# A hybrid attention and RWKV block in fp32 on one core: four products of the recurrent stage pinned behind other dense matmuls, bonus rows loaded sooner, weight casts queued behind evacuations

## The chip, the cores and the metric

The kernel runs on 1 core of one Trainium2 chip. The metric is the device time of that core in microseconds (us) for one execution; of several runs the median is given.

## The reference

One layer of a streaming encoder, on 2048 tokens with 1024 features, all in fp32:

```
h   = RMSNorm_pre(x)
P   = h @ w_in                     # columns: attention q/k/v, RWKV r/k/v + low-rank w/a/g, gates
yA  = chunk-band attention         # own chunk of 64 + 8 previous, bias on clipped distance, 8 heads of 64
yB  = RWKV-7 time mixing           # 8 heads of 64, a scan over time:
        sa    = state @ aa_t
        state = state * w_t + sa b_t^T + v_t k_t^T
        y_t   = state @ r_t
        then a group norm, a bonus (sum(r k r_k) v) and a gate g
m   = sigmoid(gA) * (yA @ proj_a) + sigmoid(gB) * (yB @ proj_b)
x   = x + RMSNorm_post(m @ w_out)
x   = x + RMSNorm_post2(relu(RMSNorm_pre2(x) @ w_up)^2 @ w_down)
```

## The kernel before

The 2048 tokens are done in four groups of 512. For each group three stages follow each other: the recurrent stage (`phase_rwkv`), attention (`phase_attention`) and the merge (`phase_merge`). Behind the fourth group come the two halves of the FFN, which the change leaves alone.

**Dense blocks.** A product of h with 128 columns of w_in is a dense block (`dense`, L108). To keep fp32 accuracy each operand is split into a high and a low part, and a block is 24 matmuls of 128x512 into one PSUM bank `psd`: eight h-high by w-high (hh,whi), eight h-low by w-high (hl,whi), eight h-high by w-low (hh,wlo). The weights of a block are loaded by SyncE's queue (`wraw`), cast to the high part by ScalarE (`whi`, L78) and subtracted to the low part by VectorE (`wlo`, L79). Each of these tiles has two buffers, and so has `psd`. So a block's cast can start only when TensorE is done with the block two back, and a block's matmuls only when the PSUM bank of the block two back has been emptied (evacuated). A group has 30 dense blocks in the recurrent stage (14 that the recurrence needs, `mix`, and 16 gates, `gate`) and 12 in attention (for each of four head pairs Q, K and V, `att_pair`), 168 in all. The branch projections (`branch`, L1086) are split in the same way, for two blocks at a time.

**The recurrent stage.** Eight heads are done as four pairs p, in two blocks b of two pairs. For each pair `rwkv_pre` forms the inputs: `mix` blends a dense block with the token before, the low-rank products `ps_z` and `ps_a` (L391, L392) give decay and rate, `ps_ss` (L450) the norm of k, `ps_v` and `ps_bk` transposes, and `ps_A` (L548) the products within chunks of 64. `rwkv_inverse` inverts small triangles on VectorE, 31 steps for both pairs at once (L584, L590, then the transposes L593 and L595). `rwkv_blocks` completes the inverse with two sets of 32x32 products, `ps_t` at L615 and at L623, which ScalarE empties to Z (L618) and XT (L628). `rwkv_trans` makes the matrices of the chunks: the transposes `ps_at` (L643), four chunks in each of two halves h, then `ps_w`, `ps_ug`, `ps_tq`, `ps_y` and the start states (L684). `rwkv_chunk` runs the recurrence over eight chunks c: `ps_st` (L699) and `ps_y` (L701) on TensorE, and the state ST (L702) on VectorE, which the next chunk needs. Nearly all these small products take turns in two PSUM buffers (`self.pa`), those of the chunks in two others (`self.pr`). `rwkv_post` norms the result (yq, var, grs, yn), adds the bonus rows `bv` (L736, L737; they were written to memory earlier) and multiplies by the gate `ps_g` (L740).

**The order.** Each engine works off one queue in order. A scheduler makes these queues; it may take instructions in another order than the program has them. In the recurrent stage the small products stand between dense matmuls, which fill TensorE while the other engines work for the small ones. Where a small product is to stand is fixed for a few of them: `place(mm, n)` notes that a product comes behind the group's dense matmul number n, and `placed` makes it an order dependency that has no semaphore (`queue_behind`). `BLOCKS` holds these numbers for the first products of L615 and L623, for both blocks b. The other small products come where the scheduler puts them. The order of SyncE's transfers, of the casts and of the evacuations follows from the scheduler too.

Of the kernel before, what the change touches and what calls it, by code (L numbers as in the profile page):

```python
# [9 lines left out]
F32 = mybir.dt.float32  # L10
BF16 = mybir.dt.bfloat16
F32R = mybir.dt.float32r
AF = mybir.ActivationFunctionType
ALU = mybir.AluOpType
# [18 lines left out]

GATES = (0, 0, 1, 0, 0, 0, 0, 1)
STEPS = (1, 2, 1, 1, 1, 1, 1, 1, 1, 1, 1, 0, 0, 2, 1)
BLOCKS = ((412, 424), (623, 632))
BONUS = {(0, 1): 138, (1, 0): 258}
SCORES = 150
DEC = math.exp(-0.5)
# [14 lines left out]
class Block:  # L54
# [50 lines left out]
    def w_in(self, col):  # L105
        return self.a["w_in"][:, col : col + P].rearrange("(k p) n -> p k n", p=P)

    def dense(self, col):  # L108

        first = bool(self.raws)  # L110
        wh, wl = self.wsplit(self.w_in(col), "w", KB, P)
        if first:
            self.queue_behind(self.high.ins, self.highs[2 - len(self.raws)])
            self.queue_behind(self.low, self.last_low)
        ps = self.pd.tile([P, G], F32, tag="d", name="psd")
        self.mm = self.mm3(ps, [(wh[:, k], wl[:, k], self.h[0][:, k], self.h[1][:, k]) for k in range(KB)], True)
        if first:
            self.queue_behind(self.mm[0], self.last_transpose)
        self.dl += self.mm
        return ps  # L120
# [235 lines left out]
    def mix(self, g, blk, out):  # L356

        nc, tp = self.nc, self.tp
        ps = self.dense(RW0 + blk * P)
        pr = tp.tile([P, G + 1], F32, tag="pr", bufs=1, name="pr")  # L360
        nc.scalar.copy(pr[:, 1 : G + 1], ps)
        nc.gpsimd.tensor_copy(pr[:, 0:1], self.carry[:, blk : blk + 1])
        nc.gpsimd.tensor_copy(self.carry[:, blk : blk + 1], pr[:, G : G + 1])
        nc.scalar.activation(out, ps, AF.Copy, scale=self.omu[:, blk : blk + 1])
        nc.vector.scalar_tensor_tensor(
            out, pr[:, 0:G], self.mu[:, blk : blk + 1], out, op0=ALU.mult, op1=ALU.add
        )
# [264 lines left out]
    def rwkv_trans(self, p, R):  # L632

        nc, xp = self.nc, self.xp
        AR, SV, XT, BR = (R[x] for x in ("AR", "SV", "XT", "BR"))
        rows = [slice(0, C), slice(C, P)]
        halves = [slice(0, 4), slice(4, 8)]

        WA = xp.tile([P, NC, 2, C], F32, tag="WA", bufs=1, name="WA")
        for h, cs in enumerate(halves):  # L640
            ps = self.pa.tile([P, 4, P], F32, tag="a", name="ps_at")
            for j in range(4):
                nc.tensor.transpose(ps[:, j], AR[:, h * 4 + j, 0:2].rearrange("p s t -> p (s t)"), self.ident)  # L643
            for par in range(2):
                nc.scalar.copy(WA[rows[par], cs, 0], ps[rows[par], :, par * C : par * C + C])
        ps = self.pa.tile([P, NC, C], F32, tag="a", name="ps_w")
        for c in range(NC):
            for par in range(2):
                ow = rows[1 - par]
                nc.tensor.matmul(ps[rows[par], c], AR[ow, c, par], SV[ow, c, par], start=True, stop=True)  # L650
        nc.scalar.copy(WA[:, :, 1], ps)
        yield

        GT = xp.tile([P, NC, C], F32, tag="GT", bufs=1, name="GT")
        for h, cs in enumerate(halves):
# [36 lines left out]
    def rwkv_chunk(self, p, c, R):  # L692
# [3 lines left out]
        ps = self.pr.tile([P, C], F32, tag="wus", name="ps_st")  # L696
        rows = [slice(0, C), slice(C, P)]
        for r in rows:
            nc.tensor.matmul(ps[r], TQ[r, c, 0], S[r], start=True, stop=True)  # L699
        for r in rows:  # L700
            nc.tensor.matmul(Y[r, c], TQ[r, c, 1], S[r], start=False, stop=c == NC - 1)  # L701
        nc.vector.scalar_tensor_tensor(  # L702
# [4 lines left out]
    def rwkv_post(self, p, R):  # L707
# [10 lines left out]
        nc.gpsimd.tensor_tensor(rs, var, self.nhalf, ALU.pow)  # L718
        yn = self.tmp("yn").rearrange("p (c t) -> p c t", t=C)
        nc.vector.tensor_tensor(yn, Y, rs[:, :, None].to_broadcast((P, NC, C)), ALU.mult)  # L720
        yield
        yf = self.tmp("yf")
        yf3 = yf.rearrange("p (c t) -> p c t", t=C)
        for h in range(2):
# [7 lines left out]
            nc.scalar.activation(  # L732
                yf3[C:P, cs], ps[:, :, C:P], AF.Identity, scale=self.gwo[:, col], bias=self.gbo[:, col]
            )
        bv = self.tmp("bv")
        nc.sync.dma_start(bv, self.bvd[p])  # L736
        self.tc.keep_in_program_order(nc.vector.tensor_tensor(yf, yf, bv, ALU.add))  # L737
        ps = self.py.tile([P, G], F32, tag="y", name="ps_g")
        self.mm3(ps, [(*(x[:, pc] for x in self.g2), *self.lg)])
# [3 lines left out]
    def gate(self, i):  # L743
        nc = self.nc
        ps = self.dense(GATE0 + i * P)
        t = self.sp.tile([P, G], F32, tag="gate", bufs=2, name="gate")
        nc.scalar.activation(t, ps, AF.Tanh, scale=0.5, bias=self.hgb[:, i : i + 1])
        nc.scalar.dma_start(self.gd[i], t)

    def phase_rwkv(self, g, quads):  # L750
# [125 lines left out]
    def att_pair(self, g, p, beside):  # L876
# [12 lines left out]
        for par in range(2):  # L889
            rw, ow = rows[par], rows[1 - par]  # L890
            nc.scalar.activation(QA[rw, par], ps[rw], AF.Copy, scale=-0.125)
            nc.scalar.activation(QB[ow, par], ps[rw], AF.Copy, scale=-0.125)
            for dst in (QB[rw, par], QA[ow, par]):
                nc.vector.scalar_tensor_tensor(  # L894
                    dst, ps[rw], -0.125, QA[rw, par].bitcast(F32), op0=ALU.mult, op1=ALU.subtract
                )
        ps = self.dense(ATT0 + HW + p * P)
        for par in range(2):
            rw, ow = rows[par], rows[1 - par]
            nc.scalar.copy(KK[rw, par, 1], ps[rw])  # L900
            nc.vector.tensor_tensor(KK[ow, par, 1], ps[rw], KK[rw, par, 1].bitcast(F32), ALU.subtract)
        ps = self.dense(ATT0 + 2 * HW + p * P)
        vf = ap.tile([P, G], F32, tag="vf", bufs=1, name="vf")
        nc.scalar.copy(vf, ps)
        pst = self.pt.tile([P, GT, P], F32, tag="t", name="ps_vt")
        for t in range(GT):
            nc.tensor.transpose(pst[:, t], vf[:, t * P : (t + 1) * P], self.ident)
# [178 lines left out]
    def branch(self, y, br, i):  # L1086

        nc, mp = self.nc, self.bp
        t = mp.tile([P, G], F32, tag="th", bufs=3, name="th")
        nc.sync.dma_start(t, self.gd[br * KB + i])  # L1090
        if i % 2 == 0:
            w = self.a[("proj_a", "proj_b")[br]][:, i * P : (i + 2) * P]
            self.bw = self.wsplit(w.rearrange("(k p) n -> p k n", p=P), "w", NP, 2 * P)
        wh, wl = (x[:, :, i % 2 * P : (i % 2 + 1) * P] for x in self.bw)
        ps = self.pd.tile([P, G], F32, tag="d", name="ps_p")
        self.mm3(ps, [(wh[:, k], wl[:, k], y[0][:, k], y[1][:, k]) for k in range(NP)])
        nc.vector.scalar_tensor_tensor(t, t, 1.0, ps, op0=ALU.add, op1=ALU.mult)  # L1097
        return t

    def phase_merge(self, g, o, op, between, beside):  # L1100
# [380 lines left out]
    def run(self):  # L1481
        tc, e = self.tc, None
        with ExitStack() as ctx, ExitStack() as mixing:
            e = mixing.enter_context
            consts = self.constants(ctx, mixing)
            advance(consts, 1)
            self.pd = ctx.enter_context(tc.tile_pool(name="pd", bufs=2, space=PSUM))
            self.wp = e(tc.tile_pool(name="w", bufs=2))
# [89 lines left out]
```

## Time and profile before

| | |
|---|---|
| time, median of 3 runs | 3269.18 us (3267.48 to 3270.03) |
| time of the profiled execution | 3272.55 us |
| its span | 3270.8 us |
| mean granted clock of TensorE | 0.993 |
| TensorE busy, matmuls | 3184.3 us |
| VectorE, ScalarE, GpSimd busy | 2239.5, 1576.9, 596.0 us |
| first group: recurrent stage's last dense matmuls to attention's first scores | near 300 to 314 us |
| second group: first recurrence, second recurrence, attention | from near 620, 719, 785 us |

Engines are named as in the profile: PE is TensorE (its matmuls), PEld TensorE's weight loads, DVE VectorE, ACT ScalarE, POOL GpSimd, SP SyncE, whose queue issues most DMAs. A row of a timeline gives the start and the time in us, engine, line and operation, out<-in, shapes, and how many instructions it stands for; what follows in brackets is the time that the engine was idle ahead of it, and the instruction whose end ended that. A row of a group of instructions (part 5 of the page) gives the busy time and the mean ns of one, and then the idle time of the engine ahead of them. A row of the windows gives for a stretch of the span the busy time of each engine, the clock that TensorE was granted (1.00 is full speed), the share of the DMA engines and GB/s. The trace counts some matmuls of the small products twice as often as the program (x32 for 16).

### The profile page before, as it was taken

What the parts mean: (1) busy time and instruction counts of PE and PEld (TensorE: products, weight loads), DVE (VectorE), ACT (ScalarE), POOL (GpSimd) and SP (SyncE); (2) the same over time, 40 slices, a digit from 0 to 9 for tenths busy, and PEclk for the clock granted to TensorE, in tenths of its full rate; (3) what the DMA queues carried; (4) which work ended last, traced back from release to release, by engine and by line L of the source; (5) the groups of instructions that cost most, each with busy time, mean ns of one, the idle gap of its engine ahead of it and who ended that gap; (6) DMA issues with size and microseconds to landing.
All of it is one profiled execution on the core that took longest, in us unless ns stands there. A gap on an engine that the chain in (4) does not pass through costs nothing. (4 is left out here: it accounts for less than half of the span.)

```text
span 3270.8 us, 50026 instructions
## 1 busy us (share of the span) xinstructions
PE 3184.3 (97%) x18913; PEld 2599.2 (79%) x18913; DVE 2239.5 (68%) x3655; ACT 1576.9 (48%) x2511; POOL 596.0 (18%) x1101
## 2 busy tenths in 40 slices
PE   8999999999999999999999999999999999999998
PEld 6777778777888777878877887888888878888887
DVE  7785666776776785776866775887656768775464
ACT  5434635445745434755434653544543444544343
POOL 2221012122112222112222110122211212120000
PEclk9999999999999999999999999999999999999999
DMA  5245373246574236565336547654777875456565
GB/s 167 85 135 172 126 241 119 72 142 235 181 234 133 88 120 234 182 205 170 94 97 206 182 156 238 226 182 166 254 278 248 290 238 193 167 177 229 193 217 175
DMA packets 432282, 592.54 MB, mean 181 GB/s; under 512 B 25300, under 2 KB 295840, under 8 KB 432040
## 3 DMA queue, kind: packets, MB, share of 16 engines
q1 hardware_dynamic: 373928, 408.94, 39.9%
q0 software_dynamic: 48896, 163.61, 13.7%
q10 hardware_dynamic: 9216, 16.78, 1.4%
q8 instruction: 149, 2.44, 0.3%
q14 instruction: 93, 0.76, 0.1%
HBM read 425.37 MB, written 167.01 MB: 181 GB/s over the span
## 5 line engine op out<-in xcount | busy, mean ns | idle before, releaser
L1409 PE MATMUL ps_dn<-fop 128*128 128x512 f32 x2688 | 611.9, 389 | 1.8 <-DVE fop L79 1.7
L1409 PEld LDWEIGHTS ps_dn<-fop 128*128 128x128 f32 x2688 | 504.0, 188 | 107.8 <-DVE fop L79 2.8
L78 ACT CAST whi<-wraw 128x1024 fp32r<-128x1024 f32 x232 | 243.5, 1050 | 392.9 <-PE psd L88 301.1
L88 PE MATMUL psd<-hh,whi 128*128 128x512 f32 x1344 | 370.3, 403 | 10.7 <-DVE QA L894 10.7
L79 DVE TENSOR_TENSOR wlo<-wraw,whi 128x1024 fp32r<-128x1024 f32 x232 | 283.0, 1220 | 133.3 <-ACT whi L78 70.0
L88 PE MATMUL psd<-hl,whi 128*128 128x512 f32 x1344 | 367.2, 401 | 0.0
L88 PE MATMUL psd<-hh,wlo 128*128 128x512 f32 x1344 | 358.4, 398 | 0.0
L88 PEld LDWEIGHTS psd<-hh,whi 128*128 128x128 f32 x1344 | 244.8, 190 | 59.8 <-issue 11.8
L88 PEld LDWEIGHTS psd<-hl,whi 128*128 128x128 f32 x1344 | 249.1, 190 | 49.5
L88 PEld LDWEIGHTS psd<-hh,wlo 128*128 128x128 f32 x1344 | 247.9, 189 | 50.8 <-issue 1.4
L79 DVE TENSOR_TENSOR fop<-xraw,fop 128x1024 fp32r<-128x1024 f32 x112 | 137.0, 1224 | 178.9 <-ACT fop L78 178.7
L78 ACT CAST fop<-xraw 128x1024 fp32r<-128x1024 f32 x112 | 117.8, 1052 | 256.4 <-PE ps_dn L1409 186.3
L1286 POOL DMA_DIRECT2D xd<-X x192 | 104.2, 545 | 384.2 <-ACT X L1283 321.9
L79 DVE TENSOR_TENSOR fop<-wdraw,fop 128x1024 fp32r<-128x1024 f32 x112 | 136.6, 1220 | 19.0 <-ACT fop L78 18.8
L78 ACT CAST fop<-wdraw 128x1024 fp32r<-128x1024 f32 x112 | 117.7, 1051 | 34.8 <-DMA wdraw<-in_w_down_dram 20.0
L947 DVE CUSTOM_DVE_ANT_0 sc<-bias,ps_s 128x640 f32<-128x640 f32 (+4 forms) x128 | 93.8, 732 | 54.2 <-PE ps_pt L958 27.1
L963 DVE TENSOR_TENSOR PTl<-ps_pt,PTh 128x640 fp32r<-128x640 f32 (+4 forms) x128 | 94.5, 738 | 32.7 <-ACT PTh L962 31.2
L78 ACT CAST s12h<-s 128x1024 fp32r<-128x1024 f32 x32 | 33.7, 1053 | 163.0 <-PE ps_u L88 163.0
L88 PE MATMUL ps_p<-yh,whi 128*128 128x512 f32 x256 | 102.6, 405 | 6.0 <-DVE th L1097 5.3
L962 ACT CAST PTh<-ps_pt 128x640 fp32r<-128x640 f32 (+4 forms) x128 | 79.7, 623 | 55.2 <-PE ps_pt L958 54.6
L952 ACT ACTIVATE sc<-sc,mn 128x640 f32<-128x640 f32 (+4 forms) x128 | 97.8, 764 | 17.4 <-DVE mn L947 15.4
L1126 PE MATMUL ps_o<-whi,mh 128*128 128x512 f32 x256 | 101.4, 396 | 1.8 <-DVE o L1137 1.8
(369 smaller groups left out, 6848.9 us busy)
## 6 DMA issues: line engine op xcount, KB each, us to landing
wraw<-in_w_in_dram SPq DMA_DIRECT2D x168, 512.0 KB
xraw<-xd SPq DMA_DIRECT2D x112, 512.0 KB
xd<-X POOLq DMA_DIRECT2D x192, 256.0 KB, 5.2
wraw<-in_w_up_dram SPq DMA_DIRECT2D x80, 512.0 KB
wdraw<-wd SPq DMA_DIRECT2D x64, 512.0 KB
wdraw<-in_w_down_dram SPq DMA_DIRECT2D x48, 512.0 KB
gd<-gate ACTq DMA_DIRECT2D x64, 256.0 KB
wd<-cmb POOLq DMA_DIRECT2D x64, 256.0 KB, 4.3
```

Source lines behind the costliest of these rows:

```text
L78: high = self.high = self.nc.scalar.copy(hi, src)
L79: self.low = self.nc.vector.tensor_tensor(lo, src, hi.bitcast(F32), ALU.subtract).ins
L88: mm.append(nc.tensor.matmul(ps, l, r, start=n == 0, stop=n == last).ins)
L947: nc.vector.tensor_tensor_reduce(sc[:, 0:n], bias[:, s0:640], pss[:, c0 : c0 + n], 1.0, 3.0e38, ALU.add, ALU.min, mn,)
L952: nc.scalar.activation(sc[:, 0:n], sc[:, 0:n], AF.Exp, scale=-1.0, bias=mn, accum_out=sm[:, col : col + 1])
L962: nc.scalar.copy(hv, pst[:, 0:nk])
L963: nc.vector.tensor_tensor(lv, pst[:, 0:nk], hv.bitcast(F32), ALU.subtract)
L1126: nc.tensor.matmul(ps[t], l[:, k, ts], r[:, k % 2], start=k == 0 and j == 0, stop=k == KB - 1 and j == 2)
L1286: nc.gpsimd.dma_start(self.xd[q][i // 2][:, i % 2], src)
L1409: nc.tensor.matmul(ps, o[:, l, k, sl], o[:, r, k], start=start and n == 0, stop=stop and n == end)
```

## The change

Five edits; what is computed stays the same, and so does the number of instructions on each engine.

1. TURNED: the first transpose of the second half of `ps_at`, for the first pair, is placed behind dense matmul 438.
2. FIFTH: the first product of chunk 4 of the first pair is placed behind dense matmul 494.
3. BLOCKS: for the second block of pairs the two sets of `ps_t` are placed behind 631 and 644 instead of 623 and 632.
4. The load of the bonus rows `bv` stands ahead of the first pause of `rwkv_post`, instead of behind the transposes that follow that pause.
5. `follow`: every evacuation of a dense block (or of a branch product) is noted in `emptied`. The cast of a block's high part is queued on ScalarE behind ScalarE's evacuation of the block three back, and the subtraction of its low part on VectorE behind VectorE's, where there is one. This is again an order without a semaphore.

```diff
-BLOCKS = ((412, 424), (623, 632))
+BLOCKS = ((412, 424), (631, 644))
+TURNED = 438
+FIFTH = 494
...
+    def follow(self):
+
+        for ins, done in zip((self.high.ins, self.low), self.emptied[-3] if len(self.emptied) > 2 else ()):
+            if done is not None:
+                self.queue_behind(ins, done.ins)
...
     def dense(self, col):
...
+        self.follow()
         ps = self.pd.tile([P, G], F32, tag="d", name="psd")
...
-        nc.scalar.activation(out, ps, AF.Copy, scale=self.omu[:, blk : blk + 1])
+        self.emptied.append((nc.scalar.activation(out, ps, AF.Copy, scale=self.omu[:, blk : blk + 1]), None))
...
             for j in range(4):
-                nc.tensor.transpose(ps[:, j], AR[:, h * 4 + j, 0:2].rearrange("p s t -> p (s t)"), self.ident)
+                mm = nc.tensor.transpose(ps[:, j], AR[:, h * 4 + j, 0:2].rearrange("p s t -> p (s t)"), self.ident)
+                if p == 0 and h == 1 and j == 0:
+                    self.place(mm, TURNED)
...
-            nc.tensor.matmul(ps[r], TQ[r, c, 0], S[r], start=True, stop=True)
+            mm = nc.tensor.matmul(ps[r], TQ[r, c, 0], S[r], start=True, stop=True)
+            if p == 0 and c == 4 and r.start == 0:
+                self.place(mm, FIFTH)
...
         nc.vector.tensor_tensor(yn, Y, rs[:, :, None].to_broadcast((P, NC, C)), ALU.mult)
+        bv = self.tmp("bv")
+        nc.sync.dma_start(bv, self.bvd[p])
         yield
...
-        bv = self.tmp("bv")
-        nc.sync.dma_start(bv, self.bvd[p])
         self.tc.keep_in_program_order(nc.vector.tensor_tensor(yf, yf, bv, ALU.add))
...
-        nc.scalar.activation(t, ps, AF.Tanh, scale=0.5, bias=self.hgb[:, i : i + 1])
+        self.emptied.append((nc.scalar.activation(t, ps, AF.Tanh, scale=0.5, bias=self.hgb[:, i : i + 1]), None))
...
-            nc.scalar.activation(QB[ow, par], ps[rw], AF.Copy, scale=-0.125)
+            act = nc.scalar.activation(QB[ow, par], ps[rw], AF.Copy, scale=-0.125)
...
-                nc.vector.scalar_tensor_tensor(
+                dve = nc.vector.scalar_tensor_tensor(
...
+        self.emptied.append((act, dve))
...
             self.bw = self.wsplit(w.rearrange("(k p) n -> p k n", p=P), "w", NP, 2 * P)
+            self.follow()
```

The evacuations of K and V and of the branch products are noted in the same way. How the rows move on the queues, at three places; a row gives the line in its own kernel, so that L643 of before is L652 of after, and so on.

The first place is TensorE's queue in the first recurrence. Before, between the two halves of the first pair's transposes:

```order
103 L623 MATMUL ps_t_1474<-XT,Z 32x32 x32
104 L643 MATMUL ps_at<-ident,AR 128x128 x4
105 L88 MATMUL psd<-hh,wlo 128x512 x4
106 L643 MATMUL ps_at<-ident,AR 128x128 x4
107 L650 MATMUL ps_w<-SV,AR 64x64 x16
```

The same place now:

```order
103 L632 MATMUL ps_t_1474<-XT,Z 32x32 x32
104 L652 MATMUL ps_at<-ident,AR 128x128 x4
105 L90 MATMUL psd<-hh,wlo 128x512 x7
106 L90 MATMUL psd<-hh,whi 128x512 x7
107 L652 MATMUL ps_at<-ident,AR 128x128 x4
108 L661 MATMUL ps_w<-SV,AR 64x64 x16
```

Fourteen dense matmuls stand between the halves where four stood. Further on the same queue, around chunk 0 (whose state is st_99 and st_100), the low-rank products and chunk 1, before:

```order
144 L391 MATMUL ps_z<-lora,whw 128x512
145 L392 MATMUL ps_z<-lora,wlw 128x512
146 L88 MATMUL psd<-hh,wlo 128x512 x4
147 L391 MATMUL ps_a<-lora,wha 128x512
148 L392 MATMUL ps_a<-lora,wla 128x512
149 L88 MATMUL psd<-hh,wlo 128x512 x3
150 L699 MATMUL ps_st<-st_99,TQ 64x64 x2
151 L701 MATMUL ps_y<-st_99,TQ 64x64 x2
152 L699 MATMUL ps_st<-st_100,TQ 64x64 x2
153 L701 MATMUL ps_y<-st_100,TQ 64x64 x2
154 L88 MATMUL psd<-hh,whi 128x512 x4
155 L699 MATMUL ps_st<-ST,TQ 64x64 x2
```

And now:

```order
146 L710 MATMUL ps_st<-st_100,TQ 64x64 x2
147 L714 MATMUL ps_y<-st_100,TQ 64x64
148 L400 MATMUL ps_z<-lora,whw 128x512
149 L401 MATMUL ps_z<-lora,wlw 128x512
150 L714 MATMUL ps_y<-st_100,TQ 64x64
151 L400 MATMUL ps_a<-lora,wha 128x512
152 L401 MATMUL ps_a<-lora,wla 128x512
153 L710 MATMUL ps_st<-ST,TQ 64x64 x2
154 L714 MATMUL ps_y<-ST,TQ 64x64 x2
155 L710 MATMUL ps_st<-ST,TQ 64x64 x2
156 L714 MATMUL ps_y<-ST,TQ 64x64 x2
157 L90 MATMUL psd<-hh,whi 128x512 x8
```

The dense matmuls that stood between these products are gone from there, and chunk 0 comes ahead of the low-rank products. Chunk 4, with FIFTH, comes 24 dense matmuls behind `ps_ss` in both kernels.

The second place is the start and the end of the second block's inverse. On TensorE the two sets of `ps_t`, before:

```order
230 L88 MATMUL psd<-hh,wlo 128x512 x8
231 L615 MATMUL ps_t_2553<-X_2451,NA 32x32 x32
232 L88 MATMUL psd<-hh,whi 128x512 x8
233 L88 MATMUL psd<-hl,whi 128x512
234 L623 MATMUL ps_t_2588<-XT,Z 32x32 x32
```

And now:

```order
227 L90 MATMUL psd<-hh,whi 128x512 x8
228 L624 MATMUL ps_t_2553<-X_2455,NA 32x32 x32
229 L90 MATMUL psd<-hl,whi 128x512 x8
230 L90 MATMUL psd<-hh,wlo 128x512 x5
231 L632 MATMUL ps_t_2588<-XT,Z 32x32 x32
```

The first set comes eight dense matmuls later, and between the two are 13 instead of 9. VectorE's queue at the start of that inverse (N is its input, T and X its steps; var and yn are the first block's norm), before:

```order
301 L715 TENSOR_REDUCE var<-yq 128x8
302 L574 STREAM_TRANSPOSE N<-NA 128x1024
303 L720 TENSOR_TENSOR yn<-ps_y,grs 128x512
304 L584 TENSOR_TENSOR T<-N,X 128x31
305 L79 TENSOR_TENSOR wlo<-wraw,whi 128x1024
306 L715 TENSOR_REDUCE var<-yq 128x8
307 L590 TENSOR_TENSOR X<-X,T 128x31
308 L79 TENSOR_TENSOR wlo<-wraw,whi 128x1024
309 L720 TENSOR_TENSOR yn<-ps_y,grs 128x512
```

And now:

```order
300 L728 TENSOR_REDUCE var<-yq 128x8
301 L583 STREAM_TRANSPOSE N<-NA 128x1024
302 L733 TENSOR_TENSOR yn<-ps_y,grs 128x512
303 L728 TENSOR_REDUCE var<-yq 128x8
304 L593 TENSOR_TENSOR T<-N,X 128x31
305 L81 TENSOR_TENSOR wlo<-wraw,whi 128x1024
306 L733 TENSOR_TENSOR yn<-ps_y,grs 128x512
307 L599 TENSOR_TENSOR X<-X,T 128x31
308 L81 TENSOR_TENSOR wlo<-wraw,whi 128x1024
```

The second variance moves ahead of a weight cast, and the second yn ahead of another.

The third place is ScalarE's queue where the first Q product of attention is emptied to QA and QB, in two halves. Before:

```order
560 L78 CAST whi<-wraw 128x1024
561 L891 ACTIVATE QA<-psd 64x512
562 L892 ACTIVATE QB<-psd 64x512
563 L78 CAST whi<-wraw 128x1024
564 L891 ACTIVATE QA<-psd 64x512
565 L892 ACTIVATE QB<-psd 64x512
566 L900 CAST KK<-psd 64x512 x2
```

And now:

```order
562 L80 CAST whi<-wraw 128x1024
563 L904 ACTIVATE QA<-psd 64x512
564 L905 ACTIVATE QB<-psd 64x512
565 L904 ACTIVATE QA<-psd 64x512
566 L905 ACTIVATE QB<-psd 64x512
567 L80 CAST whi<-wraw 128x1024
568 L914 CAST KK<-psd 64x512 x2
```

Both halves come ahead of the second cast; VectorE's four operations of L894 come ahead of the next subtraction in the same way.

More of the change, by code (lines that the diff above doesn't have):

```diff
@@ L899, in att_pair @@
             rw, ow = rows[par], rows[1 - par]
-            nc.scalar.copy(KK[rw, par, 1], ps[rw])
-            nc.vector.tensor_tensor(KK[ow, par, 1], ps[rw], KK[rw, par, 1].bitcast(F32), ALU.subtract)
+            act = nc.scalar.copy(KK[rw, par, 1], ps[rw])
+            dve = nc.vector.tensor_tensor(KK[ow, par, 1], ps[rw], KK[rw, par, 1].bitcast(F32), ALU.subtract)
+        self.emptied.append((act, dve))
         ps = self.dense(ATT0 + 2 * HW + p * P)
         vf = ap.tile([P, G], F32, tag="vf", bufs=1, name="vf")
-        nc.scalar.copy(vf, ps)
+        self.emptied.append((nc.scalar.copy(vf, ps), None))
         pst = self.pt.tile([P, GT, P], F32, tag="t", name="ps_vt")
@@ L1096, in branch @@
         self.mm3(ps, [(wh[:, k], wl[:, k], y[0][:, k], y[1][:, k]) for k in range(NP)])
-        nc.vector.scalar_tensor_tensor(t, t, 1.0, ps, op0=ALU.add, op1=ALU.mult)
+        self.emptied.append((None, nc.vector.scalar_tensor_tensor(t, t, 1.0, ps, op0=ALU.add, op1=ALU.mult)))
         return t
@@ L1485, in run @@
             consts = self.constants(ctx, mixing)
+            self.emptied = []
             advance(consts, 1)
```

## The prediction

> **What bounds the kernel now.** I read the page first, then PE's waits, then PE's clock, then what ended the longest waits. From the page, the span, the busy times, and the group of weight casts (its last column is the idle time ahead of them):
>
> ```profile
> span 3270.8 us, 50026 instructions
> PE 3184.3 (97%) x18913; PEld 2599.2 (79%) x18913; DVE 2239.5 (68%) x3655; ACT 1576.9 (48%) x2511; POOL 596.0 (18%) x1101
> L78 ACT CAST whi<-wraw 128x1024 fp32r<-128x1024 f32 x232 | 243.5, 1050 | 392.9 <-PE psd L88 301.1
> ```
>
> PE bounds it: idle only 3270.8 − 3184.3 = 86.5 us. No other engine is near. The casts wait for PE (301.1 us), not PE for the casts. So an edit pays only by taking PE's idle time, or by making PE's busy time run at full clock. PE's waits (line, what it waited for, us in total, times, longest):
>
> ```profile
> PE psd L88 <- DVE QA L894: 10.7, 4, 2.9
> PE ps_at L643 <- ACT XT L628: 9.4, 4, 2.4
> PE ps_t L615 <- DVE X L593: 6.8, 5, 1.7
> ...
> PE ps_st L699 <- DVE ST L702: 5.1, 4, 1.3
> ...
> PE ps_t L623 <- ACT Z L618: 4.7, 8, 0.8
> ```
>
> Each comes about once a group, in the four groups. Together they are 36.7 us, and all five lie where the change moves something. The other 50 us (start, merge, FFN) it leaves as they are.
>
> Some stalls cost twice: PE is at half clock behind them. First three rows of PE's timeline in dense work (8 matmuls each), then the windows behind stalls (us, then busy times by engine, then the granted clock, here 0.57 to 1.00):
>
> ```profile
> 781.30 1.98 PE L88 MATMUL psd<-hl,whi 128*128 128x512 f32 x8
> 783.11 1.98 PE L88 MATMUL psd<-hh,wlo 128*128 128x512 f32 x8
> ...
> 305.85 3.75 PE L88 MATMUL psd<-hh,whi 128*128 128x512 f32 x8 [2.90 <-DVE QA L894]
> ```
>
> ```profile
> 143.00:149.00 6.00, 5.79 (x66) 4.59 (x68) 1.23 (x1) 2.97 (x9) 0.57 (x1) 0.72 0.17 51
> 242.00:249.00 7.00, 7.00 (x112) 5.65 (x108) 0.00 (x0) 3.78 (x8) 0.54 (x1) 0.76 0.78 242
> 305.00:313.00 8.00, 7.15 (x19) 5.70 (x20) 2.07 (x3) 0.96 (x2) 0.70 (x1) 0.57 0.40 131
> ...
> 1131.00:1137.00 6.00, 5.23 (x76) 4.16 (x78) 1.23 (x1) 4.41 (x12) 0.57 (x1) 1.00 0.27 78
> ...
> 1638.00:1645.00 7.00, 6.43 (x74) 5.06 (x74) 1.23 (x1) 3.96 (x10) 0.57 (x1) 0.76 0.21 63
> 1737.00:1743.00 6.00, 5.90 (x107) 4.97 (x108) 0.00 (x1) 2.74 (x8) 0.54 (x1) 0.72 0.95 293
> ```
>
> At full clock eight dense matmuls take 783.11 − 781.30 = 1.81 us, 0.227 each; behind the QA wait of group 0 the same eight took 3.75. What a window loses is its width times (1 − clock): 6 × 0.28 = 1.68, 7 × 0.24 = 1.68, 8 × 0.43 = 3.44. The ps_at stall (143, 1638 and, alike, 625) had one in 3 of 4 groups, not at 1131; the stalls of L615 and L623 had one in 4 of 4 (first 242, last 1737); the QA stall only in group 0, a double one. That is 5.0 + 6.7 + 3.4 = 15.1 us beside the 36.7.
>
> **The change part by part**, with the times of the second group.
>
> *TURNED.* The second four transposes, PE and then ACT:
>
> ```profile
> 621.35 0.66 PE L643 MATMUL ps_at<-ident,AR 128*128 128x128 f32 x4
> 621.76 1.17 PE L88 MATMUL psd<-hh,wlo 128*128 128x512 f32 x4
> 625.29 0.66 PE L643 MATMUL ps_at<-ident,AR 128*128 128x128 f32 x4 [2.36 <-ACT XT L628]
> ```
>
> ```profile
> 623.15 1.04 ACT L78 CAST whi<-wraw 128x1024 fp32r<-128x1024 f32 x1
> 624.08 1.16 ACT L628 COPY XT<-ps_t 32x512 f32<-32x512 f32 x2
> ```
>
> They wait for the PSUM buffer that the two XT copies empty at 625.24; ACT does a whi cast ahead of these. The pin puts 14 dense matmuls between the halves where 4 stood: 10 × 0.227 = 2.27 of the 2.36 us is filled with work that was to come anyway. I leave 0.25 per group: 9.4 becomes 1.0, a gain of 8.4, and with the stall the 5.0 of half clock.
>
> What is late next: those ten were taken from between chunk 0, the two lora products (ps_z, ps_a) and chunk 1, which now follow each other with none between. PE's last ps_A, the last reading of its PSUM buffer, and the scan that stands ahead of chunk 1's ST on DVE:
>
> ```profile
> 655.93 1.16 PE L548 MATMUL ps_A<-AR,BK 64*128 64x128 f32 x8
> ```
>
> ```profile
> 658.21 0.41 DVE L566 TENSOR_TENSOR BR<-ps_A,mN 128x256 f32<-128x256 f32 x1
> ...
> 661.93 1.22 DVE L432 TENSOR_TENSOR_SCAN tw<-reset,tw 128x512 f32<-128x512 f32 x1
> ```
>
> BR ends at 658.62, 1.5 us after the ps_A; chunk 0 (16 small products, about 0.6 us) and ps_z (two of dense size, 0.45) fill some 1.1 of it before ps_a wants the buffer: 0.45. Chunk 2 has nine dense ahead of it (2.0 us), against ST behind a scan of 1.22 and three shorter operations: 0.35. The fourth pair's ps_A now follows a chunk with no dense before it and waits for a BR: 0.4. So 1.2 per group, 4.8 in all. The bounds are nothing, and three waits of the next row's size (3 × 1.29 × 4 = 15.5); I stay with the worked sum, since each part is a difference of quoted ends.
>
> *FIFTH.* PE at chunk 4, and the DVE chain that it waits for, first and last:
>
> ```profile
> 674.74 0.33 PE L699 MATMUL ps_st<-ST,TQ 64*64 64x64 f32 x4 [1.29 <-DVE ST L702]
> ```
>
> ```profile
> 666.45 0.17 DVE L452 TENSOR_SCALAR n2t<-ps_ss 128x8 f32<-128x8 f32 x1 [1.04 <-PE ps_ss L450]
> ...
> 674.32 0.47 DVE L702 SCALAR_TENSOR_TENSOR ST<-ps_st,gC,S 128x64 f32<-128x64 f32 x2
> ```
>
> Chunk 4 is pinned 8 dense later, but ST is queued behind 7.9 us of DVE work that starts at ps_ss, and ps_ss also moves 8 dense later, pulled by the ten above. There are 24 dense between ps_ss and chunk 4 in both. I count no gain; bounds 0 and the whole 5.1.
>
> *BLOCKS.* PE, then DVE's yn, then ACT:
>
> ```profile
> 718.93 1.20 PE L615 MATMUL ps_t<-X,NA 32*32 32x32 f32 x64 [1.64 <-DVE X L593]
> ...
> 723.21 0.24 PE L623 MATMUL ps_t<-XT,Z 32*32 32x32 f32 x2 [0.82 <-ACT Z L618]
> ```
>
> ```profile
> 696.64 0.69 DVE L720 TENSOR_TENSOR yn<-ps_y,grs 128x512 f32<-128x512 f32 x1 [1.81 <-POOL grs L718]
> ```
>
> ```profile
> 720.92 1.05 ACT L78 CAST whi<-wraw 128x1024 fp32r<-128x1024 f32 x1
> ...
> 722.58 0.58 ACT L618 COPY Z<-ps_t 32x512 f32<-32x512 f32 x1
> ```
>
> L615 comes 8 dense later, but the last ps_A, from which DVE's chain of the inverse starts, comes 6 later: net 2 × 0.227 = 0.45 us. The rest must come from DVE. With the casts reordered, its second variance comes ahead of a wlo cast of 1.2 us and the 1.81 us that yn waits for POOL shrink, so the chain is about 1.0 us shorter. 1.64 − 0.45 − 1.0 leaves 0.2: 6.8 becomes 0.8, a gain of 6.0. L623 gets 13 dense behind L615 instead of 9 (+0.91 us), and the cast at 720.92 goes ahead of the XT copies, so Z comes about 1 us sooner: 1.18 is covered, a gain of 4.5 of 4.7. With both the 6.7 of half clock goes. The bounds: the cover alone on L615 (1.8 instead of 6.0) and nothing of the 6.7, or all of it.
>
> *Bonus rows and the Q products.* In the order SP, DVE, ACT, PE:
>
> ```profile
> 773.85 0.51 SPq L736 DMA_DIRECT2D bv<-bvd  x1
> ```
>
> ```profile
> 779.66 0.69 DVE L737 TENSOR_TENSOR yf<-yf,bv 128x512 f32<-128x512 f32 x1 [4.45 <-DMA bv<-bvd]
> ...
> 781.06 1.22 DVE L79 TENSOR_TENSOR wlo<-wraw,whi 128x1024 fp32r<-128x1024 f32 x1
> ...
> 787.15 0.69 DVE L894 SCALAR_TENSOR_TENSOR QA<-psd,QA 64x512 fp32r<-64x512 f32 x1
> ```
>
> ```profile
> 783.31 1.05 ACT L78 CAST whi<-wraw 128x1024 fp32r<-128x1024 f32 x1 [2.42 <-PE psd L88]
> ```
>
> ```profile
> 787.99 2.08 PE L88 MATMUL psd<-hh,whi 128*128 128x512 f32 x8 [2.61 <-DVE QA L894]
> ```
>
> DVE stood 4.45 us for the bonus rows, with wlo and the emptying of the Q product queued behind; then the second half of Q stood behind the whi cast that waited for PE until 783.31, and ended at 787.84. Now the rows are issued ahead of two or three weight loads of SP, and both halves stand ahead of the next cast on ACT and on DVE. From 782.2 (the end of wlo) four operations of 0.69 end near 785, and without the 4.45 nearer 783.7; PE comes at 787.99 − 2.61 = 785.4. The wait goes: 10.7 becomes 0.5, a gain of 10.2, and the 3.4 of half clock. The weight loads are issued up to two DMA issues (0.51 each) later; they are loaded two blocks ahead and none of PE's waits names a load, so nothing is charged. If that cover were gone it is 1 us for each of two loads a group, 8 in all.
>
> *Casts behind evacuations.* No instruction is added. A cast may now stand behind an evacuation that itself waits for PE, and hold what is queued behind it on ACT and DVE. The evacuation of the block three back is due 32 dense matmuls (7.3 us) before the high part is wanted, the cast takes 1.05: some 6 us of slack. I charge nothing where they run on time. It helps where a cast waited at the head:
>
> ```profile
> 657.78 1.05 ACT L78 CAST whi<-wraw 128x1024 fp32r<-128x1024 f32 x1 [11.93 <-PE psd L88]
> ```
>
> There tw and what follows of the lora step stood behind it; now they come first.
>
> **Sum.** −8.4 − 5.0 + 4.8 − 0 − 6.0 − 4.5 − 6.7 − 10.2 − 3.4 = −39.4 us. The profiled execution took 3272.55, 3.37 over the median of 3269.18. So 3269.2 − 39.4 = 3229.8 against the median.
>
> **One rule of the Trainium skill** speaks against 15.1 us of it. The Trainium skill, page "TensorE: Matmul & The Clock Gate", section "Part 1: The HAM clock gate (the "warmup" mystery)", says that the clock drops after at least one idle window of about 3.4 us, a window that runs freely. By that, waits of 1.64 and 2.36 us are too short to cause the half clock. The trace differs so far: the windows above follow such waits. That three of four follow the ps_at stall, and not the one at 1131, fits a freely running window.
>
> **The rivals.**
>
> 1. *The chains move along.* L615 gains only its cover (1.8, not 6.0), L623 3.6 of 4.5, the half clock there stays (6.7): 4.2 + 0.9 + 6.7 = 11.8 less, 3241.6. For it: ps_A does move by 6 dense, and the ps_ss case shows the pattern. Against: a DVE idle of 1.81 that the new order should shrink.
>
> 2. *All goes.* 36.7 + 15.1 = 51.8, and the new waits are hidden: 3217.4. For it: PE still has dense work on both sides of each place. Against: ps_ss moves with chunk 4.
>
> 3. *The half clock stays.* If it belongs to the time and not to the stalls, 15.1 is lost from the sum: 3244.9. The Trainium skill's page "TensorE: Matmul & The Clock Gate" would have it so. Against: the windows quoted above all lie directly behind stalls.
>
> 4. *Slower: casts come late.* Place: every dense block, 42 a group, 168 in all. If an evacuation is held up on ACT or DVE by over 6 us, the cast behind it is late and PE waits, up to a whole cast, 1.05 us. It takes 39.4 + 6.5 = 46 us of that, 44 of the 168 blocks, to be slower by 0.2%; at 70 blocks it is 73 − 39 = 34 slower, 3303. For it: ACT's idle of 11.93 shows that a cast at the head can hold its queue so long. Against: DVE and ACT are 68% and 48% busy.
>
> 5. *Same.* Waits of 1.29 come up at all three crowded places (15.5, not 4.8), together with 1 and with the other half-clock stretches (5.0 + 3.4) staying: 39.4 − 10.7 − 11.8 − 8.4 = 8.5, so 3260.7, and within 0.2% if the Q wait keeps a fifth (2 us) as well.
>
> **How the numbers follow.** 0.2% (6.5 us) is about what a measurement of this kernel tells from no change. Chances: the forecast 0.48 (3223 to 3236), rival 1 0.21, rival 2 0.11, rival 3 0.05, all faster: 0.85. Rival 5 has 0.07, rival 4 has 0.08. The range goes from a few us below rival 2 to 3255, between rivals 1 and 5: 3211 to 3255; outside lie rivals 4 and 5 and little else.
>
> **What would show it.** In the new profile, right: PE's waits lack QA, ps_at is at most 0.5 a group, L615 and L623 together below 1 a group, ps_st still near 1.3 a group, ps_a or ps_A new at 0.3 to 0.5; clocks of 1.00 behind L623. Wrong: a wait of psd for whi or wlo (rival 4); L615 at 1.2 or more with the half clock behind it (rival 1); clock of 0.5 where PE did not stall (rival 3); waits of over 1 us at chunk 1 or 2.

## The result, and the profile after

The changed kernel takes 3245.38 us (median of 4, 3241.73 to 3250.15) against 3269.61 us (median of 4) for the kernel before: a ratio of 0.9929, 95% interval 0.9913 to 0.9945. That is 24.2 us faster, inside the range on record and above the predicted 3229.8. The profiled execution took 3241.73 us, the shortest of the four; its page begins:

```profile
span 3240.0 us, 50025 instructions
...
PE 3169.1 (98%) x18913; PEld 2588.2 (80%) x18913; DVE 2240.5 (69%) x3655; ACT 1575.2 (49%) x2511; POOL 604.0 (19%) x1101
```

The span is 30.8 us shorter. PE's busy time fell by 15.2 and its idle time by 15.6 us, from 86.5 to 70.9: about half of the gain is clock, half is waiting. PE's waits (us in total, times, longest), without that of the start:

```profile
PE ps_yt L742 <- ACT yf L747: 8.0, 4, 2.3
...
PE ps_st L710 <- DVE ST L715: 4.2, 4, 1.1
PE ps_s L956 <- DVE mn L962: 4.2, 6, 1.1
PE ps_p L90 <- ACT yh L80: 3.0, 3, 1.4
...
PE psd L90 <- ACT k L373: 1.1, 4, 0.3
...
PE ps_t L624 <- DVE X L602: 0.7, 2, 0.4
PE ps_a L400 <- DVE BR L575: 0.6, 4, 0.2
```

Of the five waits of before, those of QA, ps_at and Z (L623 of before) are gone, that of X fell from 6.8 to 0.7, that of chunk 4 from 5.1 to 4.2. The longest of these is one that before did not have: ps_yt, 8.0 us, about 2 a group. Attention's ps_s grew from 1.7 to 4.2 and the branch's wait for yh from 0.3 to 3.0.

PE's timeline at the second half of ps_at, which now stands behind 14 dense matmuls and waits for nothing:

```profile
610.94 0.66 PE L652 MATMUL ps_at<-ident,AR 128*128 128x128 f32 x4
611.35 1.89 PE L90 MATMUL psd<-hh,wlo 128*128 128x512 f32 x7
613.08 1.77 PE L90 MATMUL psd<-hh,whi 128*128 128x512 f32 x7
614.88 0.66 PE L652 MATMUL ps_at<-ident,AR 128*128 128x128 f32 x4
```

And at Q, where the dense block that waited 2.61 us follows the scores without a gap:

```profile
768.66 0.30 PE L956 MATMUL ps_s<-KK,QA 128*128 128x320 f32 x1
...
768.95 2.00 PE L90 MATMUL psd<-hh,whi 128*128 128x512 f32 x8
```

The windows of the profile after (the clock is the third number from the end): behind ps_at, behind the second ps_t set, and behind the new wait in the third group:

```profile
614.00:620.00 6.00, 5.85 (x78) 4.39 (x76) 1.03 (x1) 4.33 (x11) 1.26 (x2) 1.00 0.57 168
711.00:718.00 7.00, 6.93 (x130) 5.44 (x130) 1.88 (x3) 4.50 (x9) 1.63 (x3) 1.00 0.96 300
1194.00:1200.00 6.00, 5.95 (x23) 4.59 (x24) 5.35 (x20) 3.26 (x6) 0.54 (x1) 0.72 0.62 194
```

The first two places have full clock. The only half-clock stretch before the end of the span (1.7 us lost) follows the new wait.

Where that wait comes from can be read off the queues of the second group. PE first, then ScalarE, SyncE and VectorE:

```profile
693.49 0.63 PE L742 MATMUL ps_yt<-ident,yn 128*64 128x128 f32 x4 [1.80 <-ACT yf L747]
```

```profile
690.78 1.05 ACT L80 CAST whi<-wraw 128x1024 fp32r<-128x1024 f32 x1 [4.79 <-DMA wraw<-in_w_in_dram]
691.74 0.68 ACT L760 ACTIVATE gate<-psd,hgb 128x512 f32<-128x512 f32 x1
692.32 0.55 ACT L744 ACTIVATE yf<-ps_yt,cst 64x256 f32<-64x256 f32 x1
```

```profile
684.74 0.38 SPq L66 DMA_DIRECT2D wraw<-in_w_in_dram  x1
```

```profile
682.74 0.69 DVE L733 TENSOR_TENSOR yn<-ps_y,grs 128x512 f32<-128x512 f32 x1 [1.82 <-POOL grs L731]
683.47 1.21 DVE L81 TENSOR_TENSOR wlo<-wraw,whi 128x1024 fp32r<-128x1024 f32 x1
```

Read from the bottom: yn waits 1.82 us for GpSimd, and a wlo is queued behind it. That wlo is the last reader of a weight buffer, so the next load is issued at 684.74. The whi cast of that load waits for it until 690.78 at the head of ScalarE's queue, with a gate and the emptying of ps_yt (yf) queued behind. PE waits for yf. It is a chain through four queues.

### The profile page after: what moved, and what is told of

Read it like the earlier page. It is cut to its first block, busy times and chain, and to the rows that moved or that the text cites. A ratio compares the mean times of both kernels' runs of the same rounds, so it can differ in the third digit from the quotient of the medians.

```text
span 3240.0 us, 50025 instructions
## 1 busy us (share of the span) xinstructions
PE 3169.1 (98%) x18913; PEld 2588.2 (80%) x18913; DVE 2240.5 (69%) x3655; ACT 1575.2 (49%) x2511; POOL 604.0 (19%) x1101
## 5 line engine op out<-in xcount | busy, mean ns | idle before, releaser
L90 PE MATMUL psd<-hl,whi 128*128 128x512 f32 x1344 | 358.9, 396 | 0.0
```

The costliest lines, as they stand in the source:

```text
L90: mm.append(nc.tensor.matmul(ps, l, r, start=n == 0, stop=n == last).ins)
```

## The experiments

Each was timed against the kernel before on the same chip; since the times of the kernel before vary by a few us between the chips, ratios are compared. The expectations speak of the time of the changed kernel as 3245. Code is cut at the marks `...`.

**Is it the early bonus rows?** My first reading (theory A) blamed them: they stand ahead of weight loads on SyncE. In `bv_second`, whose edit is shown, only the last two pairs load early; in `no_V` all four load where they did before:

```diff
+        if p > 1:
             bv = self.tmp("bv")
             nc.sync.dma_start(bv, self.bvd[p])
         yield
...
+        if p < 2:
+            bv = self.tmp("bv")
+            nc.sync.dma_start(bv, self.bvd[p])
```

> The changed kernel, but the bonus rows of the first two pairs are loaded where they were before; only those of the last two pairs are loaded early. TensorE's order is the same as in the changed kernel, row for row. Theory A: the 8.0 us that TensorE waits at ps_yt for ACT yf (2.0 a group) come from the early loads, which put the weight loads later in the schedule, so that a cast waits for its DMA at the head of ScalarE's queue with gate and yf behind it; then ps_yt waits at most 0.5 us in all and the time falls by about 8 us, to 3237. Theory B: they come from TURNED, which puts TensorE ten dense matmuls ahead of ScalarE and VectorE; then ps_yt still waits 7 to 8 us and the time stays at 3245.

Measured: 3245.04 us, ratio 0.9929 [0.9915, 0.9943], and ps_yt:

```profile
PE ps_yt L743 <- ACT yf L748: 10.2, 4, 3.6
```

> The changed kernel without any early load of bonus rows (all four pairs as before). Theory A: ps_yt waits at most 0.5 us; the wait for QA stays below 2 us in all, since the casts queued behind the evacuations alone put both halves of Q ahead of the next cast; time 3237 to 3240. Theory B: ps_yt 7 to 8 us, 3245. If it was the early load that took away the wait for QA, 10.7 us of it are back: 3248 under A, 3256 under B.

Measured: 3245.3 us, ratio 0.9932 [0.9919, 0.9944]:

```profile
PE ps_yt L740 <- ACT yf L745: 9.6, 4, 4.4
...
PE psd L90 <- DVE QA L907: 0.6, 2, 0.3
```

Theory A fell: with no early load at all the wait is as long. The wait for QA stays away without the early rows.

**Is it TURNED?** `no_T` leaves out its pin:

```diff
-                if p == 0 and h == 1 and j == 0:
-                    self.place(mm, TURNED)
```

> The changed kernel without TURNED. Both theories: ps_at waits 9.4 us again, with 5 us of half clock; the waits of 1.7 us at psd<-k and ps_a go. Theory A (early loads alone): ps_yt still waits 8 us, so 3245 + 9.4 + 5 - 1.7 = 3258. Theory B, or both edits needed together: ps_yt waits nothing, 3250.

Measured: 3253.05 us, ratio 0.9954 [0.9941, 0.9967]. No row of PE's waits names ps_yt any more, and:

```profile
PE ps_at L652 <- ACT XT L637: 9.4, 4, 2.4
...
PE ps_t L624 <- DVE X L602: 4.5, 5, 1.0
```

So the wait at ps_yt comes with TURNED. Without it the order on VectorE changes too: each wlo stands ahead of the yn that waits. And the cover of BLOCKS alone does not suffice for X: 4.5 us are left there and 2.6 for Z (L615 and L623 of before).

**What are the later places of BLOCKS worth?** `no_B` restores 623 and 632:

```diff
-BLOCKS = ((412, 424), (631, 644))
+BLOCKS = ((412, 424), (623, 632))
```

> The changed kernel with BLOCKS of before. If the later places are what took the waits away: L615 and L623 wait 10 us more and the half clock behind them is back (6.7): 3262. If it was the shorter chain on VectorE (the second variance ahead of a wlo) or the cover moves along: at most 4 us more at L615 and L623, no half clock, 3249.

Measured: 3244.77 us, ratio 0.9930 [0.9918, 0.9942], with

```profile
PE ps_t L624 <- DVE X L602: 3.3, 5, 0.9
...
PE ps_t L632 <- ACT Z L627: 0.9, 3, 0.3
```

The two waits grow by 3.5 us together, not by 10, and no half clock follows them. The time does not tell the edit from nothing. For Z the reason is ScalarE's order: before, a cast (720.92) stood between the copies to XT and those to Z; here none does (XT at 709.68, Z at 711.66 us). For X it is not a shorter chain on VectorE, as the next experiments show: PE already waits 8.1 us at ps_yt, ahead of L615.

**Is the late cast the cause?** Two kernels cut the chain at one link each, while PE's order stays the same row for row. `yf_first` moves the waiting cast behind yf on ScalarE, `wlo_yn2` the wlo ahead of the waiting yn on VectorE:

```diff
         ps = self.dense(GATE0 + i * P)
+        if i == 11:
+            self.queue_behind(self.high.ins, self.yf.ins)      # yf_first
...
                 gate()
+                if i == 2:
+                    self.queue_behind(self.yn.ins, self.low)   # wlo_yn2
```

> The changed kernel, with one order added: in the recurrent stage the whi cast of gate 11 is queued on ScalarE behind the emptying of ps_yt (yf) of the first two pairs, instead of ahead of it. TensorE's order stays the same row for row. Theory C: with TURNED the weight load for this cast ends too late, the cast waits some 5 us for it at the head of ScalarE's queue, and gate and yf wait behind it; then ps_yt waits 1 us or less in all (8.0 in the changed kernel), and the time falls by some 7 us, to 3238. Theory D: TensorE is simply ahead of VectorE and ScalarE there; ps_yt waits as before, or the wait turns up at the dense block that needs the cast, and the time stays at 3245.

Measured: 3240.31 us, ratio 0.9919 [0.9906, 0.9931]. ps_yt is gone from the waits; X at L615 takes a good part back:

```profile
PE ps_t L624 <- DVE X L602: 5.6, 6, 1.2
```

Where this wait comes from changes the reading of BLOCKS. VectorE's chain of the inverse runs from N to X, for which PE waits at the first set of ps_t. Its two ends in the second group, in the kernel before (the product at 718.93, with a wait of 1.64, stands in the prediction), in `yf_first` and in the changed kernel:

```profile
688.89 2.02 DVE L574 STREAM_TRANSPOSE N<-NA 128x1024 f32<-128x1024 f32 x1
...
677.86 2.05 DVE L583 STREAM_TRANSPOSE N<-NA 128x1024 f32<-128x1024 f32 x1
707.92 1.20 PE L624 MATMUL ps_t<-X,NA 32*32 32x32 f32 x64 [1.21 <-DVE X L602]
...
676.23 2.05 DVE L583 STREAM_TRANSPOSE N<-NA 128x1024 f32<-128x1024 f32 x1
707.27 1.20 PE L624 MATMUL ps_t<-X,NA 32*32 32x32 f32 x64
```

From N to the product 30.04 us pass before and 30.06 in `yf_first` (30.08 in `no_B`). So the chain got no shorter, and PE's wait fell only from 1.64 to 1.21 us, the cover of two more dense matmuls. In the changed kernel X is ready after 30.09 us (at 706.32), but PE comes only after 31.04, since it has stood 1.80 us at ps_yt. The wait for X had moved there.

> The changed kernel, with one order added: on VectorE the second yn of the first two pairs, which waits 1.8 us for GpSimd, is queued behind the wlo of the gate before, instead of ahead of it. TensorE's order stays the same. Theory C: that wlo frees the buffer of the weight load that is late, so the load starts about 2.5 us sooner, the cast waits 2 to 3 us instead of 4.8, and ps_yt waits 2 us or less in all instead of 8.0; the time falls by 6 us, to 3239. Theory D: no change at ps_yt, 3245.

Measured: 3238.5 us, ratio 0.9918 [0.9905, 0.9932]:

```profile
PE ps_t L624 <- DVE X L602: 4.0, 6, 0.9
...
PE ps_yt L742 <- ACT yf L747: 0.3, 1, 0.3
```

On its ScalarE the cast that waited 4.79 us for its load now waits 1.69:

```profile
687.65 1.05 ACT L80 CAST whi<-wraw 128x1024 fp32r<-128x1024 f32 x1 [1.69 <-DMA wraw<-in_w_in_dram]
```

Either cut takes away the wait. So theory C holds, and theory D falls as the whole cause; that PE is ahead still sets how long the wait is, as `only_W` and `only_T` show below. By the ratios the times are 3 to 4 us below the changed kernel's, not the 6 to 7 expected, since X took back 4.9 and 3.3 of the 8.0 us; the intervals overlap its own.

**What do the queued casts do?** `no_W` leaves them out of the changed kernel, `only_W` puts them alone into the kernel before:

```diff
-        self.follow()
```

> The changed kernel without casts queued behind evacuations. If the early bonus rows suffice for Q: no wait for QA, and attention's own waits go back to those of before (ps_s for mn from 4.2 to 1.7, ps_p for yh from 3.0 to 0.3): 3240. If the queued casts carried the gain at Q or in the recurrent stage: QA 10.7 back with 3.4 of half clock, 3256. ps_yt waits about 8 us in both.

Measured: 3240.95 us, ratio 0.9921 [0.9909, 0.9934]. QA does not wait. Attention's scores are near what they were before, and the wait for yh is gone from PE's rows:

```profile
PE ps_yt L741 <- ACT yf L746: 7.5, 4, 2.1
...
PE ps_s L955 <- DVE mn L961: 2.0, 4, 0.8
```

> The kernel before with the queued casts alone. If they carry the gain at Q by themselves: QA from 10.7 to below 1, so 3267 - 10 - 3 = 3254, and L615 falls by 3 to 4 us since the second variance now stands ahead of a wlo on VectorE; 3250 with both. ps_at still 9.4, ps_yt nothing. If the early rows carried it: QA still 10.7 and 3263 to 3267.

Measured: 3260.45 us, ratio 0.9982 [0.9973, 0.9991]. QA is gone from the waits, so the casts alone suffice there as well. The rest stands as before, with 1.9 us at ps_yt:

```profile
PE ps_at L652 <- ACT XT L637: 9.4, 4, 2.4
PE ps_t L632 <- ACT Z L627: 4.7, 8, 0.8
...
PE ps_t L624 <- DVE X L602: 3.3, 5, 1.2
```

Its gain of 6 us is less than the 10.7 that QA waited, and the expected 3250 us was missed by 10. X waits 3.5 us less, but the chain from N to X is no shorter here either (30.1 us). The half clock stays, behind ps_at in three groups and behind L623 in four, and attention's waits for mn and yh grew by 5. The late cast is here too, although TURNED is not:

```profile
695.38 1.05 ACT L80 CAST whi<-wraw 128x1024 fp32r<-128x1024 f32 x1 [4.58 <-DMA wraw<-in_w_in_dram]
```

It costs little, since PE comes to ps_yt 72 dense matmuls behind the second block's last ps_A, as in the kernel before. In the changed kernel and in `only_T` it comes 66 behind.

**TURNED alone, and the changed kernel without either of the two edits at Q.** `only_T` adds two lines and the number to the kernel before; `no_VW` takes `follow` out of the changed one and puts the load of the bonus rows back to its old place:

```diff
+                if p == 0 and h == 1 and j == 0:               # only_T
+                    self.place(mm, TURNED)
...
-        self.follow()                                          # no_VW
...
-        bv = self.tmp("bv")
-        nc.sync.dma_start(bv, self.bvd[p])
         yield
```

> The kernel before with TURNED alone. ps_at waits 1 us or less (9.4 before), ps_yt waits 8 to 10 us (nothing before), QA 10.7 as before. If it is TURNED's reordering of VectorE that shortens the inverse: L615 and L623 wait 5 us or less together (11.5 before) and the half clock behind them goes: 3267 - 9 + 9 - 7 - 10 = 3250. If the later places of BLOCKS are needed: they still wait 11 us with 6.7 of half clock: 3262.

Measured: 3256.14 us, ratio 0.9967 [0.9955, 0.9979]:

```profile
PE psd L90 <- DVE QA L904: 10.7, 4, 2.9
PE ps_yt L737 <- ACT yf L742: 7.4, 4, 2.7
...
PE ps_t L623 <- DVE X L601: 3.2, 4, 1.3
```

X and Z cost 11.5 us before; with TURNED alone X costs 3.2 and Z at L623 0.3. As in `no_B`, no cast stands ahead of Z any more, and the wait at ps_yt stands ahead of X. It is 7.4 us here and 1.9 in `only_W`; the six dense matmuls that PE is ahead are 6 × 0.227 = 1.4 us a group, 5.4 in all. So that wait needs the late cast, and most of its length is PE's being ahead. The stretches of half clock behind those places are gone in three groups; in the fourth one follows X's wait of 1.33 us. New ones lie behind ps_yt and QA, and with them the time is 6 us above the expected 3250. Behind X in the fourth group:

```profile
1721.00:1727.00 6.00, 6.00 (x84) 4.62 (x82) 2.84 (x4) 3.64 (x8) 3.20 (x6) 0.72 0.65 172
```

> The changed kernel without early bonus rows and without queued casts (TURNED, FIFTH and BLOCKS remain). Either of the two edits alone kept the wait for QA away; if each does it for itself, both gone bring back 10.7 us of QA and up to 3.4 of half clock: 3245 + 10.7 + 3 = 3258. If something else in the order takes it away: QA below 1 us, 3245.

Measured: 3251.88 us, ratio 0.9956 [0.9943, 0.9969], with the whole wait at Q:

```profile
PE psd L90 <- DVE QA L906: 10.7, 4, 2.9
```

Early rows or queued casts each take the 10.7 us away; together they take it once. The time came out 6 us below the expected 3258.

**FIFTH.** The changed kernel without FIFTH alone was not run. But `only_T`, which has no FIFTH, and `no_VW`, which has it, have the same order on TensorE, ScalarE and VectorE up to the second block's ps_t, where BLOCKS differs, and both wait 4.3 us at chunk 4. `fifth_500` tries it with more cover:

```diff
-FIFTH = 494
+FIFTH = 500
```

> The changed kernel with chunk 4 behind dense matmul 500 instead of 494; ps_ss stays where it is, so 29 or 30 dense matmuls stand between them instead of 24. If chunk 4 waits for a chain of fixed length that starts at ps_ss: 6 x 0.227 = 1.4 us more cover, and its wait falls from 4.2 to 0.5 us or less in all. If the chain moves along: still 4 us. In this order a wlo also stands ahead of the yn's, so ps_yt waits 2 us or less; 3245 - 4 - 6 = 3235 under the first.

Measured: 3249.27 us, ratio 0.9949 [0.9936, 0.9962]. The expectation failed:

```profile
PE ps_t L624 <- DVE X L602: 7.8, 6, 1.7
...
PE ps_y L714 <- DVE ST L715: 4.2, 4, 1.1
```

The pin holds only the state's product. The output's product of chunk 4 reads the same state, stayed at the old place and took over the wait to the tenth of a microsecond. VectorE's order changed with it, and X waits 7.8 us again; no wait at ps_yt is left, although TURNED is in: with the wlo ahead of the yn the cast starts 14.96 us behind the last ps_A, in the changed kernel 17.00 (second group).

**The two gains together.** `best` is the changed kernel without queued casts and with the wlo ahead of the waiting yn:

```diff
-        self.follow()
...
                 gate()
+                if i == 2:
+                    self.queue_behind(self.yn.ins, self.low)
```

> The changed kernel without queued casts, with the second yn behind the wlo of the gate before. If the two gains seen one by one add (ps_yt from 8.0 to below 1, attention's ps_s and ps_p for yh from 7.2 to 2.5): 3245 - 7 - 4 = 3234. If they are one and the same or give way to other waits (L615 for X): 3238 to 3240.

Measured: 3232.1 us (3230.61 to 3233.96), ratio 0.9896 [0.9881, 0.9910]. Its interval lies below that of the changed kernel: this version beats both. Its page, and the two longest waits of PE in the recurrent stage:

```profile
span 3231.2 us, 50038 instructions
...
PE 3167.6 (98%) x18913; PEld 2587.9 (80%) x18913; DVE 2239.2 (69%) x3655; ACT 1575.2 (49%) x2511; POOL 609.0 (19%) x1101
```

```profile
PE ps_st L709 <- DVE ST L714: 4.3, 4, 1.1
...
PE ps_t L623 <- DVE X L601: 3.9, 5, 0.9
```

What is left in the recurrent stage is below 1.2 us at a time, and no stretch of half clock is found before the end of the span.

## Why the prediction was right or wrong

The sign and the order of size were right, and so was most of the sum, in the profiled executions:

| step | predicted us | measured us |
|---|---|---|
| ps_at | −8.4 | −9.4 |
| new waits at the crowded chunks | +4.8 | +1.7 |
| chunk 4 | 0 | −0.9 |
| L615, L623 | −6.0, −4.5 | −6.1, −4.7 |
| QA | −10.2 | −10.7 |
| half clock | −15.1 (9 stretches) | −17.1 (from 11 stretches in all to 1; a double one counts twice, and two of the 11 lay behind waits of the merge) |
| ps_yt | not seen | +8.0 |
| attention: ps_s, yh | not seen | +2.5, +2.7 |

**Two steps failed.** The first is in the part on the bonus rows. There weight loads were charged nothing, since "none of PE's waits names a load". PE never waits for a load by name: a cast does, and behind the cast stand the evacuations that PE waits for. With TURNED, or with the queued casts alone, VectorE has the second yn, which waits 1.8 us for GpSimd, ahead of the next wlo. That delays the wlo, and with it the next load and its cast; and TURNED brings PE to ps_yt 1.4 us sooner: 8.0 us at ps_yt. The front part shows this swap in the order. I read what the yn gains and not who is behind it.

The second is in the part on BLOCKS, where the chain of the inverse was to get "about 1.0 us shorter". It did not: from N to the product that needs X it is 30.0 us before and 30.1 now, and yn waits for GpSimd as long as it did (22.9 us in 12 waits, in both). Of the 6.0 us at L615 only the cover is real: in `yf_first` the second block's X waits 1.15 to 1.21 us a group instead of 1.64, some 1.8 less in all. That X's wait fell by 6.1 all the same is luck: the wait at ps_yt stands ahead of it and hides it. X and ps_yt together were to give −6.0 and gave +1.9.

**Casts behind evacuations** were charged nothing. In attention they cost: without them ps_s and yh wait 5.2 us less, of which the time shows some 3 (0.9921 against 0.9929, intervals that overlap). Which of the moved casts does it was not taken apart. Rival 4 had casts that come late, but looked for the wait at the dense blocks (psd for whi or wlo), and no such wait appeared; here PE waits for what stands behind the cast.

**BLOCKS** came out as summed, but not for its reasons. With TURNED alone 8 of the 11.5 us are gone from L615 and L623, Z's since ScalarE has no cast ahead of it and X's since PE stands at ps_yt; BLOCKS takes the last 3 to 4. Rival 1, by which the chains move along and L615 gains only its cover, was right on L615, with the 1.8 us that it gave it, and its 3241.6 us is nearer to the measured 3245.4 than the forecast is; the half clock that it left behind L623 is gone.

**Half clock.** In the profiled execution all of it went but one stretch, but that execution is the shortest of four, and the other three are 2 to 8 us longer. The profiles of `bv_second`, `no_V`, `no_B` and `no_W`, which have the wait at ps_yt, show two to five stretches, several at that wait: in `no_V`, at a wait of 4.37 us, a double one, which begins within the wait.

```profile
1196.00:1204.00 8.00, 5.59 (x19) 4.40 (x20) 6.60 (x20) 5.70 (x10) 0.54 (x1) 0.57 0.56 171
```

So the term was sized for waits that go, and the new wait brings part of it back, by chance of where it falls. That the spread of the four times is this is not shown, since only one of them has a profile. The mean granted clock agrees, as far as it goes: 0.998 in the shortest of the four and 0.997 in the others; in `no_V` 0.999 in the shortest of six (3239.6 us) and 0.996 in the two longest (3248.4 and 3248.7). Rival 3, near whose 3244.9 us the time came out, is refuted all the same: `best` has no wait over 1.2 us in that stage and no stretch at all.

By the Trainium skill, page "TensorE: Matmul & The Clock Gate", section "Part 1: The HAM clock gate (the "warmup" mystery)", only an idle window of about 3.4 us should drop the clock. Here it dropped behind waits of 1.3 to 2.9 us as well, in some groups and not in others; that it is chance where a wait falls agrees with the free-running window that the page describes.

**The gap.** Predicted were −39.4 us. The unseen waits take back 13.2, and the new waits at the crowded chunks were 3.1 smaller: of the three places forecast only ps_a waits (0.6), and 1.1 came up at a dense block behind chunk 1. The other steps gave 4.7 more than predicted. So the measured column adds up to −34.0, while the span fell by 30.8. The 3.2 us between them were not taken apart: the waits listed give −16.9 where PE's idle time fell by 15.6, and the half clock −17.1 where its busy time fell by 15.2. The median lies 3.6 us above the profiled execution.

## What to carry to other kernels

When a product is pinned later, follow the whole order that the scheduler makes of it: for each instruction that comes earlier, name the one that comes later, and what buffer that one frees. A load that PE never waits for can still set PE's time, through a cast at the head of a queue that also empties PSUM. A wait that falls may only have moved to a place ahead of it on the same queue: compare how long the chain behind it takes, not only the wait. And edits do not add: two of them removed the same wait at Q, and TURNED alone took most of the waits that BLOCKS was for, so each must be tried by leaving it out, not only by itself.

## What the hardware showed that was not expected

A single wait of 2 to 3 us on PE was followed by 3.4 us of half clock in some groups and not in others, at the same place of the same program. Each stretch costs up to 1.7 us, beside the wait itself. In the recurrent stage the shortest wait that one followed, with no other wait near it, was 1.33 us (`only_T`), and the longest that none followed was 3.63 us (ps_yt in `bv_second`, third group). With waits below 1.2 us none was seen in that stage, in `best`. The times of single executions spread over 8 us for the changed kernel, which has such a wait in each group (3241.7 to 3250.2), and over 3.4 us for `best`, which has none in its profile (3230.6 to 3234.0); four of each.
